# A two-layer hybrid encoder trunk: squares of two token blocks moved up, output-weight splits moved to another loop, and the next layer's norm emitted one token tile later

## The chip, the cores and the metric

One core of one Trainium2 chip runs the whole program in one launch. The metric is the device time of one execution in microseconds. The engines are TensorE (PE; PEld is its weight load), VectorE (DVE), ScalarE (ACT), GpSimd (POOL) and SyncE (SP), which issues most of the transfers.

## What is computed

The input has 1024 tokens of 1024 float32 features. Two layers are applied, each of this form (cut from the reference):

```
h = rms_norm(x, pre_g)
proj = h @ w_in
xa, ga, q_lat, kv_lat, k_rope, gb, u, v, gc = jnp.split(proj, offsets, axis=-1)
ya = rg_lru(causal_depthwise_conv(xa, conv_w, conv_b), ...) * jax.nn.silu(ga)
yb = mla(q_lat, kv_lat, k_rope, positions, ...) * jax.nn.silu(gb)
yc = spatial_gating(u, v, sgu_g, sgu_bn, sgu_w, sgu_b) * jax.nn.silu(gc)
y = jnp.concatenate([rms_norm(ya, g_a), rms_norm(yb, g_b), rms_norm(yc, g_c)], axis=-1)
return x + rms_norm(y @ w_out, post_g)
```

The first branch is a gated linear recurrence of width 384, the second an attention with 6 heads and chunk-causal mask, the third a spatial gate of width 256 that mixes tokens inside blocks of 128. All is float32.

## The kernel before

Every float32 matrix product is made of three matmuls (`mm3`, lines 123 to 126, so the trace shows lines 124, 125, 126): each operand is split into a rounded high part (ScalarE copies it, line 357 or 377) and the rest (a subtraction on GpSimd or VectorE, line 358 or 378), and high x high, high x rest and rest x high are added in PSUM. The banks of PSUM are named pw and pa; tiles in SBUF come from slot pools: F and R with 1024 floats per partition, H with 512, and Y, the array of the branches' outputs, whose rows are lent out as slots while they are free.

A layer goes through these stages; the times are those of layer 0 in the trace, layer 1 follows the same way from about 475 us.

- Prologue, 0 to 43 us. Eight blocks of 128 tokens are loaded (`load_x`), each is normalized (`prenorm`, line 325: squares with a sum on ScalarE at line 317, an inverse root on GpSimd at lines 132 and 133, a scaling on VectorE at line 328), two blocks at a time are transposed (`turn_pair`, line 331: TensorE at 339, evictions on ScalarE at 345 and VectorE at 346). Blocks 4 to 7 (`x4`) come last. The first projection groups then feed a convolution (line 436 on ScalarE, 438 and 441 on VectorE).
- Recurrence and its gates, to 105 us; u and v of the spatial branch, to 149 us. In the loop over the eight token tiles of u and v, `stage_wo` (line 620) loads a block of 128 rows of w_out in an even step and in the odd one splits it and stores both parts in a scratch tensor in device memory. Blocks 5 to 7 also get a gain (line 629).
- The spatial branch's gate, 149 to about 185 us: for each tile eight products, a tanh (716) and a release of the bank by VectorE (717). The same loop stages blocks 4 to 7 of w_out (line 721). Beside it stand the normalization of v (655), its affine step (659, 660), the spatial mixing (`sgu_mix`, 673) and, in layer 0, the rope tables on VectorE (261 to 301).
- Latents, to 215 us; the attention branch's gates, to 256 us: three blocks of gate weights by two halves of the tokens, `feat` and `gate_in` (412, 414), with keys and values made in between.
- Attention, to 400 us. The sums of squares for the attention branch's norm come in at its end (`stats`, line 512: ScalarE 517, sums 520, TensorE 524).
- Output projection, 400 to 475 us: for each of eight tiles `project` (lines 998 to 1013), a gain (1106), the norm over the row (`row_rsqrt`), scaling and residual (1110). In layer 0 the tile is normalized at once for layer 1 and, with its pair, transposed.

The order on each engine is decided by a scheduler of the framework, which reorders instructions by its own estimate of their durations; those marked with `keep` stay in program order. Each engine works through its own instructions in order. The part that stages the weights reads:

```
staged[k] = FS.take((128, 1024)), FS.take((128, 1024))
nc.sync.dma_start(out=staged[k][0], in_=A["w_out"][l, r:r + 128, :])
...
split(st, hi.bitcast(F32R), st.bitcast(F32R), G)
S_.dma_start(out=wo_dram[k][0], in_=hi)
G.dma_start(out=wo_dram[k][1], in_=st)
```

Of the kernel before, what the change touches and what calls it, by code (L numbers as in the profile page):

```python
# [17 lines left out]
NT = T // 128  # L18
# [69 lines left out]
def trunk_kernel(tc, A, out):  # L88
# [236 lines left out]
    def prenorm(xs, ns, order=lambda i: i, last=lambda i: i):  # L325
        r = row_rsqrt(xs, order=order)
        for i, (x, n) in enumerate(zip(xs, ns)):
            last(V.tensor_scalar(out=n, in0=x, scalar1=r[:, i:i + 1], scalar2=None, op0=ALU.mult))
        return ns
# [211 lines left out]
    for i in range(2):  # L541
# [3 lines left out]
                                     3: lambda: prenorm(xn[3:4], xn[3:4], keep)})  # L545
    turn_pair(0, xn[2:], hT, 1, FS)
    turn_params(prow)
    ws[1].split(keep)
    prenorm(x4[:2], x4[:2], keep)
    xn, xs = x4, FS  # L550

    for l in range(DEPTH):
# [35 lines left out]
        if l == 0:  # L588
            prenorm(xn[2:], xn[2:], last=keep)
# [30 lines left out]
        def stage_wo(n):  # L620

            k, r = n // 2, W_ROWS[n // 2]
            if n % 2 == 0:
                staged[k] = FS.take((128, 1024)), FS.take((128, 1024))
                nc.sync.dma_start(out=staged[k][0], in_=A["w_out"][l, r:r + 128, :])
                return
            st, hi = staged.pop(k)
            if k >= 5:
                S_.activation(st, st, AF.Copy, scale=bgain(r // 128))
            split(st, hi.bitcast(F32R), st.bitcast(F32R), G)  # L630
# [80 lines left out]
        for t in range(NT):  # L711
# [9 lines left out]
            stage_wo(8 + t)  # L721
# [327 lines left out]
        for m in range(3):  # L1049
# [6 lines left out]
            for half in range(2):  # L1056
                ps = bank("P1")
                feat(ps, hT, w, 0, half)
                gate_in(ps, YB + m, half)
                if m == 2:  # L1060
# [32 lines left out]
        xn = []  # L1093
        for t in range(NT):
            ts = slice(t * 128, (t + 1) * 128)
            xo = load_x(src, t)
            yh, yl, z = started.pop(t, None) or project(t, 0, 5)
            cols = tile_cols(t)
# [8 lines left out]
            r = row_rsqrt([z], cols)  # L1107
# [5 lines left out]
            if l + 1 < DEPTH:  # L1113
                if t < 4:
                    xn += prenorm([z], [xo])
                    if t % 2:
                        turn_pair(l + 1, xn, hT, t // 2, FS)
                        xn = []
                else:
                    if t == 4:  # L1120
                        for y in yhalf:
                            YS.lend(y)
                        ws = {0: W(l + 1, 0, 256, 4)}
                        xs = YS
                    n = YS.take((128, 2, 512))
                    xn += prenorm([z], [n])
                    FS.give(xo)
            else:
                FS.give(xo)
# [27 lines left out]
```

## Time and profile before

| | |
|---|---|
| median of 3 runs | 928.41 us (928.18 to 929.45) |
| the profiled execution | 924.58 us |
| its span | 922.8 us |
| mean granted TensorE clock | 0.988 of full speed |
| busy PE / PEld | 879.5 / 777.6 us |
| busy DVE / ACT / POOL | 569.9 / 519.8 / 411.6 us |
| moved by DMA | 86.93 MB, 94 GB/s on average |

The profiled execution is one run with records; the span is what the records cover, and 1.8 us of its time lie outside of it. In a row of the timeline the first number is the start, the second the duration, and the brackets at the end give the idle time of the engine ahead of the instruction and what ended it. Matmuls are pipelined, so a row's duration is longer than the distance to the next one. The granted clock is 1.00 at 2.4 GHz and 0.50 at 1.2 GHz.

### The profile page before, as it was taken

What the parts mean: (1) busy time and instruction counts of PE and PEld (TensorE: products, weight loads), DVE (VectorE), ACT (ScalarE), POOL (GpSimd) and SP (SyncE); (2) the same over time, 40 slices, a digit from 0 to 9 for tenths busy, and PEclk for the clock granted to TensorE, in tenths of its full rate; (3) what the DMA queues carried; (4) which work ended last, traced back from release to release, by engine and by line L of the source; (5) the groups of instructions that cost most, each with busy time, mean ns of one, the idle gap of its engine ahead of it and who ended that gap; (6) DMA issues with size and microseconds to landing.
All of it is one profiled execution on the core that took longest, in us unless ns stands there. A gap on an engine that the chain in (4) does not pass through costs nothing. (4 is left out here: it accounts for less than half of the span.)

```text
span 922.8 us, 13671 instructions
## 1 busy us (share of the span) xinstructions
PE 879.5 (95%) x5078; PEld 777.6 (84%) x5078; DVE 569.9 (62%) x1083; ACT 519.8 (56%) x1032; POOL 411.6 (45%) x460
## 2 busy tenths in 40 slices
PE   6799998999999999989999999989989999999996
PEld 5698887998889889867888888889978999988786
DVE  4457965755589897454456488434555989863322
ACT  6445844544767778444544386344466877755312
POOL 3320037464045568384743000666530567656822
PEclk9799999999999999999999999999999999999998
DMA  7200447322000253022324022762200015221322
GB/s 275 56 24 23 137 148 241 134 107 59 14 1 1 93 183 115 23 89 93 116 94 123 1 80 86 292 221 110 59 14 0 1 47 194 80 70 47 127 101 92
DMA packets 45079, 86.93 MB, mean 94 GB/s; under 512 B 8824, under 2 KB 26836, under 8 KB 45012
## 3 DMA queue, kind: packets, MB, share of 16 engines
q1 hardware_dynamic: 35796, 52.50, 17.8%
q0 software_dynamic: 6912, 25.17, 7.8%
q10 hardware_dynamic: 2304, 8.39, 2.3%
q8 instruction: 40, 0.66, 0.3%
q14 instruction: 27, 0.22, 0.1%
HBM read 60.88 MB, written 25.17 MB: 93 GB/s over the span
## 5 line engine op out<-in xcount | busy, mean ns | idle before, releaser
L124 PE MATMUL pw<-R,R 128*128 128x512 f32 (+1 forms) x704 | 258.8, 370 | 10.8 <-DVE Y L441 6.7
L125 PE MATMUL pw<-R,R 128*128 128x512 f32 (+1 forms) x704 | 253.0, 360 | 0.0
L126 PE MATMUL pw<-R,R 128*128 128x512 f32 (+1 forms) x704 | 252.7, 360 | 0.3 <-POOL R L378 0.3
L124 PE MATMUL pa<-R,R 128*128 128x512 f32 (+3 forms) x540 | 187.8, 349 | 9.6 <-DVE Y L717 4.4
L125 PE MATMUL pa<-R,R 128*128 128x512 f32 (+3 forms) x540 | 186.0, 345 | 0.0
L126 PE MATMUL pa<-R,R 128*128 128x512 f32 (+3 forms) x540 | 184.7, 345 | 0.0
L124 PEld LDWEIGHTS pw<-R,R 128*128 128x128 f32 x704 | 134.5, 192 | 31.3 <-issue 6.9
L126 PEld LDWEIGHTS pw<-R,R 128*128 128x128 f32 x704 | 134.5, 191 | 19.1 <-POOL R L378 0.9
L125 PEld LDWEIGHTS pw<-R,R 128*128 128x128 f32 x704 | 135.1, 192 | 17.4
L124 PEld LDWEIGHTS pa<-R,R 128*128 128x128 f32 x540 | 102.1, 189 | 20.6 <-DVE Y L717 4.6
L949 POOL TENSOR_SCALAR F<-F,ring 128x128 f32<-128x128 f32 (+3 forms) x96 | 72.8, 763 | 89.1 <-DVE ring L948 87.7
L126 PEld LDWEIGHTS pa<-R,R 128*128 128x128 f32 x540 | 101.8, 189 | 9.9
L125 PEld LDWEIGHTS pa<-R,R 128*128 128x128 f32 x540 | 102.2, 189 | 8.6
L358 DVE TENSOR_TENSOR R<-pa,R 128x512 fp32r<-128x512 f32 (+1 forms) x120 | 73.9, 630 | 16.7 <-ACT R L357 15.7
L947 ACT ACTIVATE F<-pw,ring 128x128 f32<-128x128 f32 (+3 forms) x96 | 71.1, 743 | 20.8 <-DVE ring L945 18.4
L945 DVE TENSOR_REDUCE ring<-pw 128x1 f32<-128x128 f32 (+3 forms) x96 | 71.6, 749 | 11.3 <-PE pw L938 10.7
L378 POOL TENSOR_TENSOR R<-F,R 128x1024 fp32r<-128x1024 f32 (+1 forms) x23 | 51.1, 2229 | 61.1 <-ACT R L377 36.9
L357 ACT ACTIVATE R<-pa 128x512 fp32r<-128x512 f32 (+1 forms) x120 | 63.8, 554 | 19.2 <-PE pa L969 17.6
L978 PE MATMUL pa<-R,R 128*128 128x256 f32 x480 | 72.1, 288 | 0.5 <-DVE R L358 0.5
L978 PEld LDWEIGHTS pa<-R,R 128*128 128x128 f32 x480 | 63.4, 190 | 3.6 <-DVE R L358 1.1
L969 PE MATMUL pa<-ident,F 128*128 128x128 f32 x432 | 63.6, 273 | 0.4 <-DVE R L358 0.3
L1106 POOL TENSOR_TENSOR F<-F,F 128x1024 f32<-128x1024 f32 (+2 forms) x20 | 39.3, 1966 | 47.6 <-DVE F L1013 47.4
(302 smaller groups left out, 1357.5 us busy)
## 6 DMA issues: line engine op xcount, KB each, us to landing
F<-in_w_in SPq DMA_DIRECT2D x26, 512.0 KB, 4.4
F<-in_x SPq DMA_DIRECT2D x12, 512.0 KB, 4.2
F<-in_w_out SPq DMA_DIRECT2D x9, 512.0 KB, 3.6
F<-x SPq DMA_DIRECT2D x8, 512.0 KB, 4.4
Y<-in_w_out SPq DMA_DIRECT2D x7, 512.0 KB, 4.4
x<-F SPq DMA_DIRECT2D x7, 512.0 KB
out_y<-F SPq DMA_DIRECT2D x7, 512.0 KB
F<-in_w_in SPq DMA_DIRECT2D x7, 352.0 KB, 4.4
```

What stands on the lines that cost most here:

```text
L124: PE.matmul(ps, lhsT=sh, rhs=mh, start=start, stop=False)
L125: PE.matmul(ps, lhsT=sh, rhs=ml, start=False, stop=False)
L126: PE.matmul(ps, lhsT=sl, rhs=mh, start=False, stop=stop)
L357: S_.activation(h, src, AF.Copy)
L358: (eng or G).tensor_tensor(out=lo, in0=src, in1=h.bitcast(F32), op=ALU.subtract)
L378: (eng or self.eng).tensor_tensor(out=lo, in0=st, in1=h.bitcast(F32), op=ALU.subtract)
L945: V.tensor_reduce(out=mx, in_=sv, axis=AX.XY, op=ALU.max, negate=True)
L947: S_.activation(p[:, 0:n].rearrange("p (a b) -> p a b", a=sv.shape[1]), sv, AF.Exp, bias=mx, accum_out=sm)
L949: G.tensor_scalar(out=p[:, 0:n], in0=p[:, 0:n], scalar1=rs, scalar2=1.0, op0=ALU.mult, op1=ALU.mult)
L969: PE.transpose(pv[:, c, i * 128:(i + 1) * 128], p[i][:, b * 128:(b + 1) * 128], ident)
L978: PE.matmul(o, lhsT=sv, rhs=pt[:, part, c * 256:(c + 1) * 256], start=(b == 0 and part == 0), stop=(b == nb - 1 and part == 1))
L1106: G.tensor_tensor(out=zgf[:, c], in0=zf[:, c], in1=gf[:, c], op=ALU.mult)
```

## The change

1. `prenorm` is taken apart into `row_rsqrt` and `scale_rows`. The squares of blocks 4 and 5 now come between the transposes of the two pairs of the prologue, their scaling after the parameters' turning; blocks 6 and 7 keep the squares' place and are scaled after the first projection group. These instructions keep program order.
2. `stage_wo` takes the second slot only when it splits; blocks 4 to 7 are loaded and split in the loop of the attention gates (steps 0 to 3 load, steps 1 to 4 split), no more in the spatial gate's loop. Gain and copy keep program order.
3. In the output projection, what belongs to the next layer's norm moves into `finish(t)`, which is called one tile later, behind that tile's first five products; the row norm keeps program order. The loan of Y's rows and the first weight load of the next layer come a little earlier in tile 4.

```
@@ -322,10 +322,12 @@
                                    op1=ALU.add)
         return rsqrt(ms[:, 0:len(xs)], len(xs))
 
-    def prenorm(xs, ns, order=lambda i: i, last=lambda i: i):
-        r = row_rsqrt(xs, order=order)
+    def scale_rows(xs, ns, r, order=lambda i: i):
         for i, (x, n) in enumerate(zip(xs, ns)):
-            last(V.tensor_scalar(out=n, in0=x, scalar1=r[:, i:i + 1], scalar2=None, op0=ALU.mult))
+            order(V.tensor_scalar(out=n, in0=x, scalar1=r[:, i:i + 1], scalar2=None, op0=ALU.mult))
+
+    def prenorm(xs, ns, order=lambda i: i):
+        scale_rows(xs, ns, row_rsqrt(xs, order=order))
         return ns
 
     def turn_pair(l, xn, hT, pair, slots, then={}, order=lambda i: i):
@@ -543,10 +545,12 @@
     ws[0].split(eng=V, n=1)
     turn_pair(0, xn[:2], hT, 0, FS, {0: lambda: ws[0].split(keep), 1: lambda: prenorm(xn[2:3], xn[2:3], keep),
                                      3: lambda: prenorm(xn[3:4], xn[3:4], keep)})
+    r4 = row_rsqrt(x4[:2], order=keep)
     turn_pair(0, xn[2:], hT, 1, FS)
     turn_params(prow)
+    scale_rows(x4[:2], x4[:2], r4, keep)
     ws[1].split(keep)
-    prenorm(x4[:2], x4[:2], keep)
+    r6 = row_rsqrt(x4[2:], order=keep)
     xn, xs = x4, FS
 
     for l in range(DEPTH):
@@ -586,7 +590,7 @@
 
         group(0, 0)
         if l == 0:
-            prenorm(xn[2:], xn[2:], last=keep)
+            scale_rows(xn[2:], xn[2:], r6, keep)
         hT.append(new_hT())
 
         if l:
@@ -621,13 +625,14 @@
 
             k, r = n // 2, W_ROWS[n // 2]
             if n % 2 == 0:
-                staged[k] = FS.take((128, 1024)), FS.take((128, 1024))
-                nc.sync.dma_start(out=staged[k][0], in_=A["w_out"][l, r:r + 128, :])
+                staged[k] = FS.take((128, 1024))
+                nc.sync.dma_start(out=staged[k], in_=A["w_out"][l, r:r + 128, :])
                 return
-            st, hi = staged.pop(k)
+            st, hi = staged.pop(k), FS.take((128, 1024))
             if k >= 5:
-                S_.activation(st, st, AF.Copy, scale=bgain(r // 128))
-            split(st, hi.bitcast(F32R), st.bitcast(F32R), G)
+                keep(S_.activation(st, st, AF.Copy, scale=bgain(r // 128)))
+            keep(S_.activation(hi.bitcast(F32R), st, AF.Copy))
+            G.tensor_tensor(out=st.bitcast(F32R), in0=st, in1=hi, op=ALU.subtract)
             S_.dma_start(out=wo_dram[k][0], in_=hi)
             G.dma_start(out=wo_dram[k][1], in_=st)
             FS.give(st)
@@ -718,7 +723,6 @@
                                    op0=ALU.add, op1=ALU.mult)
             HS.give(th)
             drain(2)
-            stage_wo(8 + t)
         w.give()
         drain(100)
         HS.give(sg)
@@ -1057,6 +1061,11 @@
                 ps = bank("P1")
                 feat(ps, hT, w, 0, half)
                 gate_in(ps, YB + m, half)
+                step = 2 * m + half
+                if 0 < step < 5:
+                    stage_wo(7 + 2 * step)
+                if step < 4:
+                    stage_wo(8 + 2 * step)
                 if m == 2:
                     for p in hT[half]:
                         for t in p:
@@ -1090,11 +1099,34 @@
         gpost = load_bcast(A["post_norm_g"][l])
         if l + 1 < DEPTH:
             hT = [new_hT()]
-        xn = []
+        xn, zs = [], {}
+
+        def finish(t):
+
+            z, xo = zs.pop(t)
+            if l + 1 < DEPTH:
+                n = xo if t < 4 else YS.take((128, 2, 512))
+                xn.extend(prenorm([z], [n], keep))
+                if t < 4 and t % 2:
+                    turn_pair(l + 1, xn, hT, t // 2, FS)
+                    xn.clear()
+                if t >= 4:
+                    FS.give(xo)
+            else:
+                FS.give(xo)
+            FS.give(z)
+
         for t in range(NT):
             ts = slice(t * 128, (t + 1) * 128)
             xo = load_x(src, t)
             yh, yl, z = started.pop(t, None) or project(t, 0, 5)
+            if t:
+                finish(t - 1)
+            if t == 4 and l + 1 < DEPTH:
+                for y in yhalf:
+                    YS.lend(y)
+                ws = {0: W(l + 1, 0, 256, 4)}
+                xs = YS
             cols = tile_cols(t)
             project(t, 5, 8, (yh, yl, z))
             RS.give(yh)
@@ -1104,30 +1136,14 @@
             for c in cols:
                 c = slice(*c)
                 G.tensor_tensor(out=zgf[:, c], in0=zf[:, c], in1=gf[:, c], op=ALU.mult)
-            r = row_rsqrt([z], cols)
+            r = row_rsqrt([z], cols, keep)
             for c in ((0, 512), (512, 1024)) if t == NT - 1 else cols:
                 c = slice(*c)
                 V.scalar_tensor_tensor(out=zf[:, c], in0=zgf[:, c], scalar=r, in1=xf[:, c], op0=ALU.mult, op1=ALU.add)
                 nc.sync.dma_start(out=(x1_dram if l == 0 else out[0])[ts, c], in_=zf[:, c])
             FS.give(zg)
-            if l + 1 < DEPTH:
-                if t < 4:
-                    xn += prenorm([z], [xo])
-                    if t % 2:
-                        turn_pair(l + 1, xn, hT, t // 2, FS)
-                        xn = []
-                else:
-                    if t == 4:
-                        for y in yhalf:
-                            YS.lend(y)
-                        ws = {0: W(l + 1, 0, 256, 4)}
-                        xs = YS
-                    n = YS.take((128, 2, 512))
-                    xn += prenorm([z], [n])
-                    FS.give(xo)
-            else:
-                FS.give(xo)
-            FS.give(z)
+            zs[t] = z, xo
+        finish(NT - 1)
         for p in wo:
             for t in p:
                 RS.give(t)
```

ScalarE in the prologue (L317 are the squares, H is their scratch output, F and Y hold the blocks; L345 or L347 evicts transposes, L377 or L379 splits weights, L436 or L438 starts the convolution). Before:

```order
L317 ACTIVATE H_143,ring<-F_139 128x1024
L345 ACTIVATE R_101<-pa_66,pg 128x256
L345 ACTIVATE R_103<-pa_67,pg 128x256
...
L377 ACTIVATE R_113<-F_140 128x1024
L377 ACTIVATE R_115<-Y 128x1024
L317 ACTIVATE H_142,ring<-Y 128x1024
L317 ACTIVATE H_143,ring<-Y 128x1024
L317 ACTIVATE H_141,ring<-Y 128x1024
L317 ACTIVATE H_142,ring<-Y 128x1024
L436 ACTIVATE Y<-pw_63,par 128x512
```

And now:

```order
L317 ACTIVATE H_143,ring<-F_139 128x1024
L317 ACTIVATE H_142,ring<-Y 128x1024
L317 ACTIVATE H_143,ring<-Y 128x1024
L347 ACTIVATE R_101<-pa_66,pg 128x256
...
L379 ACTIVATE R_113<-F_140 128x1024
L379 ACTIVATE R_115<-Y 128x1024
L317 ACTIVATE H_142,ring<-Y 128x1024
L317 ACTIVATE H_143,ring<-Y 128x1024
L438 ACTIVATE Y<-pw_63,par 128x512
```

Two squares of blocks held in Y stand ahead of the eight evictions of pair 1, and two, not four, between the weight splits and the convolution.

TensorE in the spatial gate of layer 0 (pw_64 is the gate product of tile 2, pa_65 behind it the spatial mixing). Before:

```order
L126 MATMUL pa_66<-R_115,R_108 128x256
L124 MATMUL pw_64<-R_116,R_101 128x256
L125 MATMUL pw_64<-R_114,R_101 128x256
L126 MATMUL pw_64<-R_116,R_102 128x256
...
L124 MATMUL pa_65<-R_128,R_130 128x256
L125 MATMUL pa_65<-R_129,R_130 128x256
L126 MATMUL pa_65<-R_128,R_130 128x256
L124 MATMUL pw_64<-R_116,R_103 128x256
```

And now:

```order
L126 MATMUL pa_66<-R_115,R_108 128x256
L124 MATMUL pw_64<-R_116,R_101 128x256
L125 MATMUL pw_64<-R_114,R_101 128x256
L126 MATMUL pw_64<-R_116,R_102 128x256
...
L126 MATMUL pw_64<-R_115,R_108 128x256
L124 MATMUL pa_65<-R_128,R_130 128x256
L125 MATMUL pa_65<-R_129,R_130 128x256
L126 MATMUL pa_65<-R_128,R_130 128x256
L124 MATMUL pa_67<-R_125,R_101 128x352
```

The mixing on pa_65, which waits for VectorE's release of that bank (L717, now L722), stands behind 24 matmuls on pw_64 instead of 6.

TensorE at the end of attention in layer 0 (L978 or L982 is attention's last value product, pw the early output projection, L524 or L526 the second sum of squares). Before:

```order
L978 MATMUL pa_68<-R_106,R_118 128x256 x3
L124 MATMUL pw_64<-R_125,R_103 128x512
L125 MATMUL pw_64<-R_126,R_103 128x512
L126 MATMUL pw_63<-R_123,R_108 128x512
...
L126 MATMUL pw_63<-R_101,R_108 128x512
L524 MATMUL pa_66<-ones,H_142 128x1 x4
L126 MATMUL pw_64<-R_125,R_108 128x512
```

And now:

```order
L982 MATMUL pa_68<-R_106,R_118 128x256 x4
L124 MATMUL pw_63<-R_123,R_103 128x512
L125 MATMUL pw_63<-R_109,R_103 128x512
L124 MATMUL pw_64<-R_125,R_103 128x512
L125 MATMUL pw_64<-R_126,R_103 128x512
L526 MATMUL pa_66<-ones,H_143 128x1 x4
L126 MATMUL pw_63<-R_123,R_108 128x512
```

The sum of squares follows the last value product after 4 matmuls; before, 30 stood between the two.

## Rows read from the trace of the kernel before

**Rows 1.** The page, part 1: busy time per engine, share of the span, instructions.

```profile
PE 879.5 (95%) x5078; PEld 777.6 (84%) x5078; DVE 569.9 (62%) x1083; ACT 519.8 (56%) x1032; POOL 411.6 (45%) x460
```

**Rows 2.** TensorE's timeline: start us, us, engine, line, instruction, [idle before <-releaser].

```profile
34.68 0.77 PE L124 MATMUL pw<-R,R 128*128 128x512 f32 x1 [6.69 <-DVE Y L441]
...
160.03 0.58 PE L124 MATMUL pa<-R,R 128*128 128x256 f32 x1 [4.40 <-DVE Y L717]
...
414.93 0.66 PE L339 MATMUL pa<-ident,F 128*128 128x128 f32 x4 [3.92 <-DVE F L328]
...
416.13 0.79 PE L124 MATMUL pw<-R,R 128*128 128x512 f32 x1 [0.54 <-ACT F L1011]
...
499.35 0.39 PE L124 MATMUL pa<-R,R 128*128 128x256 f32 x1 [1.60 <-DVE R L346]
```

**Rows 3.** By stretch: length, busy (count) PE PEld DVE ACT POOL, granted clock, DMA share.

```profile
31.00:40.00 9.00, 5.32 (x13) 4.24 (x14) 5.51 (x11) 0.00 (x0) 0.69 (x1) 0.50 0.01 2
...
160.00:170.00 10.00, 9.97 (x60) 9.97 (x61) 9.31 (x30) 4.69 (x7) 1.36 (x2) 0.83 0.41 131
...
410.00:420.00 10.00, 5.54 (x19) 4.00 (x18) 3.99 (x4) 5.01 (x8) 6.99 (x8) 0.83 0.42 157
...
600.00:620.00 20.00, 17.42 (x133) 16.72 (x132) 7.42 (x16) 8.54 (x13) 14.09 (x11) 1.00 0.64 220
...
670.00:690.00 20.00, 16.61 (x92) 13.98 (x91) 12.19 (x29) 12.58 (x28) 7.07 (x6) 1.00 0.06 15
```

**Rows 4.** ScalarE's timeline, 16 to 31 us.

```profile
19.73 3.03 ACT L345 ACTIVATE R<-pa,pg 128x256 fp32r<-128x256 f32 x8 [2.86 <-PE pa L339]
...
24.50 1.10 ACT L317 ACTIVATE H<-Y 128x1024 bf16<-128x1024 f32 x1
...
28.66 1.49 ACT L436 ACTIVATE Y<-pw,par 128x512 f32<-128x512 f32 x2
```

**Rows 5.** VectorE's timeline, 24 to 41 us.

```profile
31.03 0.15 DVE L438 COPY tails<-pw 128x3 f32<-128x3 f32 x1
```

**Rows 6.** VectorE's timeline, 149 to 163 us: two rope rows and the release.

```profile
157.70 1.69 DVE L275 TENSOR_SCALAR Y<-Y 128x128 f32<-128x128 f32 x1
...
159.56 0.41 DVE L717 SCALAR_TENSOR_TENSOR Y<-H,pa 128x256 f32<-128x256 f32 x1
...
160.94 0.23 DVE L275 TENSOR_SCALAR Y<-Y 128x128 f32<-128x128 f32 x1
```

**Rows 7.** GpSimd's timeline, 149 to 161 us.

```profile
157.64 1.67 POOL L378 TENSOR_TENSOR R<-F,R 128x704 fp32r<-128x704 f32 x1
```

**Rows 8.** VectorE's timeline, 162 to 170 us.

```profile
163.39 1.38 DVE L655 TENSOR_SCALAR F<-F,mv,ring 128x256 f32<-128x256 f32 x4
...
164.89 1.22 DVE L659 TENSOR_TENSOR F<-F,H 128x1024 f32<-128x1024 f32 x1
```

**Rows 9.** By line, duration ns min/median/max: subtraction, copy, gain.

```profile
L358 POOL TENSOR_TENSOR F<-F,F x6: 2378/2406/2410, 131.9 to 631.3; 128x1024 fp32r<-128x1024 f32 x6
...
L357 ACT ACTIVATE F<-F x6: 1058/1061/1064, 129.8 to 626.3; 128x1024 fp32r<-128x1024 f32 x6
...
L629 ACT ACTIVATE F<-F,par x3: 1152/1155/1157, 165.0 to 616.1; 128x1024 f32<-128x1024 f32 x3
```

**Rows 10.** By stretch: the attention gates of layer 0.

```profile
215.00:256.00 41.00, 41.00 (x208) 35.23 (x207) 20.74 (x42) 24.73 (x46) 7.27 (x8) 1.00 0.07 16
```

**Rows 11.** TensorE's timeline: end of attention and the second statistics, layer 0.

```profile
398.96 0.62 PE L978 MATMUL pa<-R,R 128*128 128x256 f32 x3 [0.24 <-DVE R L358]
...
406.27 0.94 PE L524 MATMUL pa<-ones,H 128*128 128x1 f32 x8
```

**Rows 12.** VectorE's sum L520: the timeline at 402 us, and by line.

```profile
402.61 2.11 DVE L520 TENSOR_TENSOR H<-H,H 128x512 f32<-128x512 f32 x1 [0.70 <-ACT H L517]
...
L520 DVE TENSOR_TENSOR H<-H,H x8: 683/1292/2108, 374.0 to 856.8; 128x512 f32<-128x512 f32 x8
```

**Rows 13.** DMA issues from 0 to 20 us: KB each, median us to landing.

```profile
Y<-in_x SPq DMA_DIRECT2D x4, 512.0 KB, 8.8
```

## The prediction

> **What bounds the kernel now.** I began with the busy times: TensorE is busy for 879.5 us of a span of 922.8 [rows 1], so 43.3 us of idling is all that any reordering can save, apart from time at the lower clock. The second view is TensorE's own timeline, for the gaps. The five rows of [rows 2] are long ones, each with its releaser: 6.69 us ahead of the convolution's release in layer 0, 4.40 us in the spatial-gate projection, 3.92 and 0.54 us in the output projection, 1.60 us at the start of layer 1. The rows by stretch add two more places in layer 1: the gate projection of the spatial branch idles 20.00 - 17.42 = 2.58 us, the start of the attention gates 20.00 - 16.61 = 3.39 us [rows 3]. The third thing to see is in the same rows: after the three longest gaps the granted clock stood at 0.50 (31 to 40 us) or averaged 0.83 over ten microseconds, that is the 1.2 GHz level for a part of them, while the stretches with gaps of 1.6 us or less show 1.00. At 0.83 a gap costs another 0.17 x 10 = 1.7 us, because TensorE advances at half speed.
>
> The profiled execution took 924.58 us, 3.83 below the median of 928.41. All terms below are differences; I subtract them from the median.
>
> **Squares of blocks 4 and 5 (layer 0, prologue).** ScalarE idles 2.86 us before the transposes' evictions of pair 1 at 19.73. The four squares begin at 24.50 and the convolution's first instruction follows them at 28.66, so a square takes 4.16 / 4 = 1.04 us [rows 4]. Two fit into the gap (2.1 of 2.86 us). Then only two stand ahead of the convolution, which can start when the last matmul ends, at 34.68 - 6.69 = 27.99. VectorE's first convolution copy comes one such instruction (1.49 / 2 us) later, near 28.8, instead of at 31.03 [rows 5], since the scalings in front of it are done early too. Every later step moves with it: **-2.2 us**. The clock stays low until about 40 whatever restarts at 34.68; a shorter gap could bring it back sooner or never lower it, worth up to half of the 5.3 us from 34.68 to 40. Bounds: 0 (the data come too late for the gap) and -4.9.
>
> **Output weights 4 to 7 (layer 0).** Their load, gain, copy, subtraction and stores leave the spatial-gate loop. Of the 4.40 us gap there, VectorE's release came at 159.56, behind rope operations. One of these took 1.69 us at 157.70, the same line at 160.94 took 0.23 [rows 6]; the long one ran exactly beside GpSimd's weight split of 157.64 to 159.31 [rows 7]. The Trainium skill, GPSIMD Engine Reference, section Specifications, says GpSimd's path to SBUF is shared with VectorE and contended when VectorE runs in a two-port mode or reads two SBUF inputs. The row agrees: 1.69 against 0.23 us; by that rule the moved subtractions take such holds with them to the new stage, by the bare instruction times they don't (a rival below). In the new order TensorE has 24 matmuls on bank pw ahead of the spatial mixing instead of 6: 18 more at 17.42 / 133 = 0.13 us [rows 3] are 2.4 us of cover. But VectorE now has four normalizations (1.38 us) and an affine product (1.22 us) [rows 8] ahead of its first releases. I take 2.0 us of gaps left and the clock kept up: 4.4 + 1.7 - 2.0 = **-4.1**, between -6.1 (no gap) and 0 (a gap as long as before). Layer 1 loses the same work, from the stretch with 2.58 us idle: **-1.5**, between -2.6 and 0.
>
> **The same work in the attention gates' loop.** ScalarE gets per layer four copies of 1.06 and three gains of 1.15 us: 7.7 us. GpSimd gets four subtractions of 2.41 us, 9.6 us [rows 9], and the issues of four stores. In layer 0 TensorE has no idle time there, ScalarE is busy 24.73 and GpSimd 7.27 of 41 us [rows 10]. There is room (32.4 of 41), and three banks between TensorE and its readers cover a single delay. I take +0.5 for layer 0. Layer 1's counterpart has 3.39 us of gaps, which another order of VectorE and ScalarE may shorten or repeat; I take -1.0. Together **-0.5**, between -4 and +4.
>
> **The norm one tile later.** The gaps of 3.92 and 0.54 us and the clock behind them (1.7) go: 6.2 us. The next wait comes from the order. Before, the second statistics product (L524) stood 30 matmuls of the early projection behind attention's last value product (L978); it ran at 406.27 and waited for nothing. Now four stand between, and the last L978 ended at 398.96 + 0.62 = 399.58 [rows 11]. The 30 took (406.27 - 399.58) / 30 = 0.22 us each, so four end near 400.5; its operand comes from VectorE's sum L520, which ends at 402.61 + 2.11 = 404.7 [rows 12]. That is a new gap of 4.2 to 4.4 us, longer than the one that lowered the clock: 4.4 + 1.7 = 6.1 lost against 6.2 saved. When the held projection is over (43 matmuls, some 10 us, and the clock), near 417, the scaled tile that ended the old gap at 414.93 is there and the transposes wait for nothing. So **0**. This sum of VectorE takes between 0.68 and 2.11 us [rows 12]; if short, and the clock holds, the term is -6.2 + 3.0 = -3.2. If one more reader is late it is +1.5.
>
> **Start of layer 1.** Transposes of the last pair are split and 24 weight matmuls put ahead, which covers the 1.60 us and smaller waits; the scaling of tile 7 now stands behind the gates' weight split on VectorE, a wait of about 1.7 us in exchange. I take **-0.6**, between -2.4 and +1. Attention is only reshuffled: 0, within 1.5 either way, judged by the single waits of a few tenths there. The end of layer 1 keeps its order. The loads of the output weights move on SyncE's queue into a stage with 7% DMA share [rows 10]; the third block of gate weights now stands behind two of them, but two blocks' matmuls come before it is needed: 0. On GpSimd's queue the last subtraction stands behind a memset that waits for TensorE and ahead of the first scaling of attention: at most 2.4 us and an issue, within the bounds of the gates' term.
>
> Sum: -2.2 - 4.1 - 1.5 - 0.5 + 0 - 0.6 = -8.9, so 928.4 - 8.9 = **919.5 us**.
>
> **Rivals.**
> - *Deeper.* The clock never falls at the new statistics gap (-1.7), comes back early in the prologue (-2.7) and the spatial gate has no gap (-2.0): 919.5 - 6.4 = 913.1. For it: gaps up to 1.6 us left the clock at 1.00. Against: 3.92 us lowered it. Chance 0.07.
> - *VectorE's queue in the spatial gate.* The normalizations and both affine steps (1.38 + 1.22 + about 1.2 = 3.8 us) all end before the first release; the gap stays 3.8 and lowers the clock: the term is 4.4 - 3.8 = -0.6 instead of -4.1: 923.0. For it is the order, against it the 2.4 us of cover. Chance 0.13.
> - *The squares don't fit.* The loads of x need 8.8 us to landing under full DMA [rows 13]; if blocks 4 and 5 come after 18, ScalarE, which runs in order, holds up the evictions of pair 1. With the term at +1 instead of -2.2 it gives 922.7. Chance 0.05.
> - *Slower.* GpSimd's eight subtractions hold VectorE in the gates' loop as the split held L275, and in-order VectorE holds the releases of TensorE's banks and the first scores. Fully exposed they cost 8 x 2.41 = 19.3 us. From 8.9 / 19.3 = 46% exposed the change loses; with two thirds exposed the time is 919.5 + 12.9 = 932.4. For it: the wide rope row. Against: VectorE idles half of this stage, and only instructions like weight scalings are open to it, not the gates' own. Chance 0.13.
> - *No change.* The new waits, each sized above, come out at their upper bounds (0 for the spatial gate, +4 for the gates' loop, -2.2 and -1.5 kept): within 0.2%, which is about what a measurement of this kernel can tell from none. Chance 0.07.
>
> **Numbers.** The forecast has the remaining 0.55. Faster by over 0.2%: 0.55 + 0.07 + 0.13 + 0.05 = 0.80; the same 0.07; slower 0.13. For the range, the bounds of the prologue (2.7 down, 2.2 up) and of the spatial gate (2.0 down, 4.1 up) weigh most. Below it reaches to 912.5, the deeper case with 0.6 more; above to 929.0, past the no-change case, leaving out the slower one and a little at the bottom.
>
> **What would show it.** Right: TensorE's gap at the convolution is near 4.5 us, restarting near 32.5; no gap over 2 us in the spatial gate and no 0.50 there; a gap of 4 us in front of the second L526 (was L524) with the low clock behind it, and none at the transposes. Wrong: gaps over 1 us in the attention gates of layer 0, or POOL subtractions with VectorE instructions of 2 us beside them; a gap at the pair-1 evictions; the first scores later than before relative to the last gate matmul.

## The result, and the profile after

The changed kernel takes 943.03 us in the median of four runs (940.34 to 944.29); the kernel before takes 928.29 in four (925.91 to 929.45). The ratio is 1.0145, 95% interval 1.0121 to 1.0169: **slower by 14.7 us, where 919.5 was forecast and 929.0 was the upper end of the range**.

The profiled execution of the changed kernel took 944.29 us (span 942.5), that of before 924.58. So the two traces differ by 19.7 us, 5 more than the medians, and single steps below are good to an us or two, those of layer 1 to less (see behind the table). The page of the changed kernel, part 1, answers to [rows 1]:

```profile
span 942.5 us, 13695 instructions
PE 889.7 (94%) x5078; PEld 784.1 (83%) x5078; DVE 585.8 (62%) x1083; ACT 522.8 (55%) x1032; POOL 409.0 (43%) x460
```

TensorE has the same 5078 matmuls and is 10.2 us longer busy: more of them ran at the lower clock (a mean granted clock of 0.982; it was 0.988). Its idle time grew from 43.3 to 942.5 - 889.7 = 52.8 us. VectorE has the same 1083 instructions as before and is 585.8 - 569.9 = 15.9 us longer busy: instructions of the same kinds and sizes take longer. That is the odd number of this page, and the experiments turn on it.

In the lines of the changed kernel, L359 and L360 (for weights L379 and L380) are the copy and the subtraction of a split, L634 and L635 those of a staged block of w_out. L810 and L811 split the transposed latents, L888 and L889 the keys; L994 is the product that ends a unit of attention.

The longer waits of TensorE's timeline (start, duration, engine, line, instruction, idle before and its releaser), after; the first, second and sixth stand where the first three of [rows 2] stood:

```profile
32.76 0.77 PE L124 MATMUL pw<-R,R 128*128 128x512 f32 x1 [5.11 <-DVE Y L443]
157.37 0.39 PE L124 MATMUL pa<-R,R 128*128 128x256 f32 x1 [2.44 <-DVE Y L722]
228.86 0.66 PE L802 MATMUL pa<-ident,F 128*128 128x128 f32 x4 [1.17 <-DVE R L811]
260.00 0.69 PE L124 MATMUL pa<-R,R 128*128 128x384 f32 x1 [4.08 <-DVE R L889]
363.52 0.30 PE L973 MATMUL pa<-ident,F 128*128 128x128 f32 x1 [2.75 <-DVE R L360]
412.65 0.33 PE L526 MATMUL pa<-ones,H 128*128 128x1 f32 x1 [3.97 <-DVE H L522]
686.78 0.50 PE L124 MATMUL pa<-R,R 128*128 128x512 f32 x1 [1.16 <-DVE Y L416]
```

By stretch (from:to, length, busy and count of PE, PEld, DVE, ACT, POOL, granted clock, DMA share, GB/s), behind these waits:

```profile
255.00:266.00 11.00, 6.92 (x25) 6.21 (x23) 8.19 (x14) 6.04 (x16) 3.49 (x4) 0.69 0.24 95
360.00:370.00 10.00, 7.22 (x43) 6.87 (x43) 8.46 (x17) 5.44 (x13) 6.59 (x12) 0.83 0.44 150
410.00:420.00 10.00, 7.35 (x22) 6.17 (x23) 4.20 (x4) 2.72 (x5) 8.93 (x10) 0.66 0.04 14
680.00:700.00 20.00, 18.29 (x82) 14.46 (x82) 12.04 (x23) 12.72 (x21) 6.64 (x6) 0.91 0.49 151
815.00:830.00 15.00, 12.15 (x76) 10.96 (x75) 11.32 (x23) 9.63 (x23) 10.59 (x17) 0.89 0.46 141
```

The waits at 260.00 and 363.52, and the low clock at 815 to 830, have no counterpart before. The averages below 1.00 show that TensorE worked a part of each stretch at 1.2 GHz.

**Where the time went.** Both kernels issue the same matmuls. I give each matmul its shape's spacing at full clock and add up ("by equal work"); the sum is the same in both, some 855 to 860 us by how the spacing is read, and the time at which each kernel reaches the same part of it shows where it fell behind:

| step | forecast | by the traces |
|---|---|---|
| prologue | -2.2 | -2.6 |
| spatial gate and latents, layer 0 | -4.1 | -0.9 |
| attention gates and start of attention, layer 0 | +0.5 | +10.1 |
| attention, layer 0 | 0 | +2.5 |
| norm one tile later | 0 | +0.4 |
| start of layer 1 | -0.6 | -0.5 |
| layer 1 through its spatial gate | -1.5 | -1.9 |
| attention gates, layer 1 | -1.0 | +4.2 |
| attention, layer 1 | 0 | +6.4 |
| end of layer 1 | 0 | +2.0 |
| sum | -8.9 | +19.7 |

The profiled execution of before was quick in layer 1. Experiment 11 has the same order of instructions there, and by equal work falls 3.4 us behind it between 605 and 693. The rows of layer 1 are good to no more than that.

### The profile page after: what moved, and what is told of

Its sections match the earlier page's. It is cut to its first block, busy times and chain, and to the rows that moved or that the text cites. A ratio compares the mean times of both kernels' runs of the same rounds, so it can differ in the third digit from the quotient of the medians.

```text
span 942.5 us, 13695 instructions
## 1 busy us (share of the span) xinstructions
PE 889.7 (94%) x5078; PEld 784.1 (83%) x5078; DVE 585.8 (62%) x1083; ACT 522.8 (55%) x1032; POOL 409.0 (43%) x460
## 4 chain that ended last, share of the span: by engine, by line
PE 50%; DVE 11%; ACT 6%; issue 3%; DMA 2%; POOL 1%; DVEq 0%; POOLq 0%; ACTq 0%; SPq 0%
PE pw L124 9%; PE pw L126 9%; PE pw L125 9%; PE pa L982 5%; PE pa L973 4%; PE pa L124 4%; PE pa L125 4%; PE pa L126 4%; DVE R L360 2%; DMA F<-in_w_in 2%; DVE ring L949 1%; ACT F L951 1%; DVE Y L994 1%; PE pw L942 1%; ACT R L359 1%
## 5 line engine op out<-in xcount | busy, mean ns | idle before, releaser
L124 PEld LDWEIGHTS pa<-R,R 128*128 128x128 f32 x540 | 102.8, 191 | 25.4 <-DVE R L889 5.6
L126 PEld LDWEIGHTS pa<-R,R 128*128 128x128 f32 x540 | 102.7, 191 | 10.1
L125 PEld LDWEIGHTS pa<-R,R 128*128 128x128 f32 x540 | 103.0, 191 | 8.9
L380 POOL TENSOR_TENSOR R<-F,R 128x1024 fp32r<-128x1024 f32 (+1 forms) x23 | 51.8, 2255 | 84.2 <-ACT R L379 61.0
L360 DVE TENSOR_TENSOR R<-pa,R 128x512 fp32r<-128x512 f32 (+1 forms) x120 | 73.6, 629 | 22.1 <-ACT R L359 20.9
L982 PE MATMUL pa<-R,R 128*128 128x256 f32 x480 | 75.8, 294 | 0.1
L359 ACT ACTIVATE R<-pa 128x512 fp32r<-128x512 f32 (+1 forms) x120 | 62.9, 553 | 18.6 <-PE pa L973 16.0
L973 PE MATMUL pa<-ident,F 128*128 128x128 f32 x432 | 65.5, 276 | 4.9 <-DVE R L360 4.8
L982 PEld LDWEIGHTS pa<-R,R 128*128 128x128 f32 x480 | 66.5, 196 | 3.1 <-DVE R L360 0.7
L1138 POOL TENSOR_TENSOR F<-F,F 128x1024 f32<-128x1024 f32 (+2 forms) x20 | 39.2, 1962 | 54.1 <-DVE F L1017 52.9
```

What stands on the lines that cost most here:

```text
L124: PE.matmul(ps, lhsT=sh, rhs=mh, start=start, stop=False)
L125: PE.matmul(ps, lhsT=sh, rhs=ml, start=False, stop=False)
L126: PE.matmul(ps, lhsT=sl, rhs=mh, start=False, stop=stop)
L359: S_.activation(h, src, AF.Copy)
L360: (eng or G).tensor_tensor(out=lo, in0=src, in1=h.bitcast(F32), op=ALU.subtract)
L380: (eng or self.eng).tensor_tensor(out=lo, in0=st, in1=h.bitcast(F32), op=ALU.subtract)
```

## The experiments

**What VectorE did at the two new waits.** VectorE's timeline before the wait of 260.00, after:

```profile
255.20 0.68 DVE L889 TENSOR_TENSOR R<-pa,R 64x512 fp32r<-64x512 f32 x1 [1.59 <-ACT R L888]
256.80 2.42 DVE L360 TENSOR_TENSOR R<-H,R 128x512 fp32r<-128x512 f32 x1 [0.92 <-ACT R L359]
259.25 0.69 DVE L889 TENSOR_TENSOR R<-pa,R 64x512 fp32r<-64x512 f32 x1
...
261.36 0.69 DVE L360 TENSOR_TENSOR R<-H,R 128x512 fp32r<-128x512 f32 x1
```

and GpSimd's, the same stretch:

```profile
256.33 2.34 POOL L635 TENSOR_TENSOR F<-F,F 128x1024 fp32r<-128x1024 f32 x1 [3.03 <-ACT F L634]
258.62 0.30 POOL L977 MEMSET R<- 128x256 f32 x1
```

L360, a split of 512 columns, takes 0.69 us at 261.36 and 2.42 at 256.80, where the moved subtraction of GpSimd (L635) runs from 256.33 to 258.67. The held L360 ends at 259.22, that is 0.55 after it. L889 stands behind it on VectorE, and TensorE waits for L889. The hold makes 1.7 of the 4.08 us. On ScalarE the moved copy stands right ahead of L359, the copy that this L360 waited for:

```profile
255.19 1.06 ACT L634 ACTIVATE F<-F 128x1024 fp32r<-128x1024 f32 x1
256.15 0.61 ACT L359 ACTIVATE R<-H 128x512 fp32r<-128x512 f32 x1
```

The wait of 363.52, VectorE then GpSimd, after:

```profile
358.14 0.42 DVE L991 SCALAR_TENSOR_TENSOR H<-pa,H 64x256 f32<-64x256 f32 x1
358.59 3.72 DVE L994 TENSOR_TENSOR Y<-Y,H 64x256 f32<-64x256 f32 x1
362.23 0.54 DVE L949 TENSOR_REDUCE ring<-pw 128x1 f32<-128x384 f32 x1
362.70 1.13 DVE L360 TENSOR_TENSOR R<-pa,R 128x512 fp32r<-128x512 f32 x2
```

```profile
358.69 2.10 POOL L953 TENSOR_SCALAR F<-F,ring 128x896 f32<-128x896 f32 x2
360.77 1.25 POOL L360 TENSOR_TENSOR R<-H,R 128x512 fp32r<-128x512 f32 x1
361.98 0.60 POOL L1024 DMA_DIRECT2D R<-wo5h  x1
```

And the same product in the kernel before, VectorE:

```profile
353.42 0.42 DVE L990 TENSOR_TENSOR Y<-Y,H 64x256 f32<-64x256 f32 x1
```

The product of attention's unit 16 (counted from 0) took 0.42 us and takes 3.72 beside three GpSimd instructions on end, until their end at 362.02 and 0.29 more. A reduction and the L360 that TensorE waits for stand behind it. In layer 1 the same product took 3.02 us, beside the same three:

```profile
817.10 3.02 DVE L994 TENSOR_TENSOR Y<-Y,H 64x256 f32<-64x256 f32 x1
```

It was not touched by the change: the scheduler, which had a new set of instructions to place upstream, set it beside that train.

The theory **A** of what follows: part 2 of the change (the output weights 4 to 7) is the whole loss, by VectorE instructions held for the length of the GpSimd instructions beside them. Rival **B**: by the copies and gains on ScalarE, which stand ahead of its own evictions (at 225.84 a moved copy of 1.05 us runs just ahead of L810, on which L811 and the wait of 228.86 rest; the copy at 255.19 above is another). Rival **C**: by the new order in attention as such, whatever lies beside what.

**1. Without the move.** Parts 1 and 3 alone; the staging of blocks 4 to 7 as before:

```
-                step = 2 * m + half
-                if 0 < step < 5:
-                    stage_wo(7 + 2 * step)
-                if step < 4:
-                    stage_wo(8 + 2 * step)
...
             drain(2)
+            stage_wo(8 + t)
```

> The changed kernel with part 2 undone: output weights 4 to 7 are staged in the spatial gate's loop again, parts 1 (squares) and 3 (norm later) stay. All theories that blame part 2 expect the attention start and attention as before: prologue -2.6 us, output stage +0.4, start of layer 1 -0.5, so 925 to 926 us against 928.3 before. If parts 1 or 3 cost the time, it stays above 935.

Measured: 927.52 us (12 runs) beside 929.65 for before, ratio 0.9974 (0.9958 to 0.999). By equal work it is 2.0 us ahead of before all the way from the gates to the output projection. There the wait for the transposes is still 3.89 us long (at 412.93), where 3.92 stood before [rows 2]: part 3 by itself did nothing to it.

**2. The move alone.** The kernel before with part 2.

> The kernel before with part 2 alone. If part 2 makes the whole loss, 943.0 + 2.7 = 945 to 946 us; if it needs part 1 or 3 beside it, 928 to 935.

Measured: 945.33, ratio 1.0162 (1.0127 to 1.0197). Part 2 is the whole loss, and more: 1.0162 x 0.9974 = 1.0136, within the interval of the full change. TensorE waits 3.97 us for the second sum of squares here as in the full change: it is part 2 that put this wait in the place of the transposes', by way of the scheduler. The time fits A, B and C alike. Part 2 also makes the copies of all eight blocks keep program order and takes the second slot later; no run separates that from the move.

**3. The staged subtractions on VectorE.** This frees the gates' stage of GpSimd's long instructions. The line serves all eight blocks of a layer, so the four that were not moved go to VectorE too, sixteen in all.

```
-            G.tensor_tensor(out=st.bitcast(F32R), in0=st, in1=hi, op=ALU.subtract)
+            V.tensor_tensor(out=st.bitcast(F32R), in0=st, in1=hi, op=ALU.subtract)
```

> The changed kernel with the staged subtraction on VectorE (some 1.2 us each) instead of GpSimd; the order in attention is unchanged. Theory A (GpSimd's subtraction of 2.4 us holds VectorE): the VectorE rows of 2.4 us in the attention gates' loop shrink to 0.7, the gap at attention's start in layer 0 falls from 4.1 to 2.2 us or less and the clock stays up there, 3 to 5 us gained in layer 0 and 1 to 3 in layer 1: 935 to 939 us. Theory B (ScalarE's copies and gains ahead of the key evictions): the gap stays near 4 us, 942 to 945. Theory C (the new order in attention): its loss of 2.7 and 6.9 us inside attention stays in both cases.

Measured: 942.05, ratio 1.0132 (1.0104 to 1.0161): a miss in time; the interval overlaps that of the change. The hold is gone, as VectorE's timeline shows at the same place:

```profile
256.48 1.22 DVE L635 TENSOR_TENSOR F<-F,F 128x1024 fp32r<-128x1024 f32 x1 [0.46 <-ACT F L634]
257.63 0.68 DVE L360 TENSOR_TENSOR R<-H,R 128x512 fp32r<-128x512 f32 x1
258.34 0.69 DVE L889 TENSOR_TENSOR R<-pa,R 64x512 fp32r<-64x512 f32 x1
```

L360 is back at 0.68 us and the wait of 4.08 is gone. But one grew upstream, on TensorE, and lowered the clock there:

```profile
229.67 0.55 PE L802 MATMUL pa<-ident,F 128*128 128x128 f32 x3 [1.96 <-DVE R L811]
227.00:240.00 13.00, 10.46 (x34) 7.87 (x34) 7.20 (x8) 6.28 (x10) 3.02 (x2) 0.74 0.77 226
```

The product of unit 16 is still held, for 3.68 us. By equal work the place gains 6.4 us against the change, and the chain upstream (L810, L811) loses 3.3 more. So the subtraction's hold was real, but a good half of what it cost in that one place was paid at another.

**4. The copies and gains on GpSimd.** This takes all the moved work off ScalarE, and the copies of the four blocks that were not moved with it.

```
-                keep(S_.activation(st, st, AF.Copy, scale=bgain(r // 128)))
-            keep(S_.activation(hi.bitcast(F32R), st, AF.Copy))
+                G.tensor_scalar(out=st, in0=st, scalar1=bgain(r // 128), scalar2=None, op0=ALU.mult)
+            G.tensor_copy(hi.bitcast(F32R), st)
```

> The changed kernel with gain and copy of the moved weights on GpSimd instead of ScalarE; the order of attention in layer 0 is unchanged. Theory B: with ScalarE freed of 7.7 us the gap at attention's start in layer 0 falls from 4.1 to below 2 us. Theory A: GpSimd works longer, VectorE is held at more places, the gap is as long or longer, and the time is 943 us or more.

Measured: 945.22 (two runs), ratio 1.0167 (1.0127 to 1.0207): no gain. But the sign that had been set for B did come: at attention's start in layer 0, where the change has the wait of 4.08 us, TensorE has none over 0.2, and by equal work the 7 us lost there are gone. The time stayed up because other waits grew; the longest stands in the spatial gate of layer 0, where GpSimd now also has the copy of a block that was not moved:

```profile
167.10 0.58 PE L124 MATMUL pa<-R,R 128*128 128x256 f32 x1 [5.04 <-DVE Y L722]
```

L360 is held less at attention's start too (1.62 us at 252.87), since GpSimd's subtractions come at other times. So this run doesn't tell A from B at that place, and it can't be read as "B has no part": it shows that GpSimd is no better home for the copies.

**5. Unit 16's product on GpSimd.** One number leaves the table of products that VectorE takes.

```
-Y_ON_V = (2, 4, 5, 6, 8, 9, 13, 14, 16, 19, 20, 21, 23)
+Y_ON_V = (2, 4, 5, 6, 8, 9, 13, 14, 19, 20, 21, 23)
```

> The changed kernel with attention's product of unit 16 on GpSimd instead of VectorE (0.74 us there); the order of the rest in attention is unchanged. In the changed kernel this product took VectorE 3.72 us in layer 0 and 3.02 in layer 1, beside back-to-back GpSimd work, against 0.42 before. Theory A (GpSimd holds VectorE): the gaps behind it (2.75 us at 361, 1.07 and 1.36 at 816 to 821) and the two clock falls of 3.4 us vanish, 7 to 9 us: 934 to 937 us. Theory C (the new order as such): the gaps stay, 941 to 944.

Measured: 933.47 (10 runs), ratio 1.0043 (1.0026 to 1.0061). Against the change that is 943.03 - 933.47 = 9.6 us, from one product of 0.42 us that is run once per layer. In attention of layer 0 every engine's order is otherwise the same up to 369, so C is out there. By stretch, the places of both holds:

```profile
355.00:370.00 15.00, 14.66 (x106) 13.47 (x105) 12.83 (x29) 13.02 (x31) 14.45 (x21) 1.00 0.45 142
810.00:830.00 20.00, 18.71 (x132) 17.09 (x131) 15.63 (x34) 15.91 (x36) 16.29 (x23) 1.00 0.40 132
```

The clock stays at 1.00 in both. By equal work 4.2 us come back at the first place and 3.4 at the second. Behind the second, from 827, the scheduler changed the order as well, and the 2.0 us that the table has at the end of layer 1 are gone there. The wait at the start of attention is still there (4.47 us at 261.31). This is the strongest run for A.

**6. Both, 3 and 5.**

> Both: the staged subtraction on VectorE and the product of unit 16 on GpSimd, part 2 otherwise as in the changed kernel. If the two holds add up: 942.0 - 7 to 9 = 933 to 936 us, and what is left against the kernel before lies in the attention gates' loop, about 4 to 6 us. If the first gives way to another wait: 938 or more.

Measured: 931.52 (10 runs), ratio 1.0022 (1.0007 to 1.0037), 2.0 us less than experiment 5, which was measured beside it. So of the 15.9 us that part 2 costs (1.0145 against 0.9974) the two edits take away 11.4, most of it by the product. What is left against experiment 1, 1.0022 - 0.9974 = 0.5% or 4.5 us (give or take 2), comes from neither hold. An estimate from the traces says that it comes from no more holding at all. I add up what VectorE's instructions took above the median of their kind, shape and tiles: 27 us before, 30 in experiment 1, 42 after the change, 43 in experiment 2, 34 in 3 and in 5, and 28 here.

Where the rest stands, by equal work: layer 0 loses 4.2 us in the gates' loop, where L802 waits 1.96 us at 228.24 for L811, and ahead of L811 ScalarE has the moved copy (1.05 us) and VectorE the moved subtraction (1.23 us). Layer 1 loses 2.2 in its gates' loop and 3.9 in attention up to 815, in small waits. B names a part of this; so may the eight subtractions that this edit needlessly put on VectorE. It was not taken apart further.

Experiments 7 to 10 start from experiment 1 and ask whether the two waits that part 2 and part 3 were aimed at can be had in another way.

**7. Subtractions of blocks 4 to 7 on VectorE, in their old place.**

```
-            split(st, hi.bitcast(F32R), st.bitcast(F32R), G)
+            split(st, hi.bitcast(F32R), st.bitcast(F32R), V if k >= 4 else G)
```

> Part 2 undone (as in the run without the move), and the subtractions of blocks 4 to 7, in the spatial gate's loop, on VectorE instead of GpSimd; attention's order is unchanged. Theory A: the release of the bank there no longer waits behind held rope rows, the gap of 4.4 us falls below 2.5 and the clock stays up: 3 to 5 us, 922.5 to 924.5 us against 927.5. If the gap comes from ScalarE or the tanh, it stays: 927 to 929, or 1 to 2 more for VectorE's longer work.

Measured: 930.22 (12 runs), ratio 1.0007 (0.9987 to 1.0027): a miss; the wait became longer. One of VectorE, then GpSimd, then TensorE:

```profile
156.07 1.76 DVE L261 CAST ring<-pos_i 128x8 f32<-128x8 int32 x1
156.11 1.68 POOL L380 TENSOR_TENSOR R<-F,R 128x704 fp32r<-128x704 f32 x1
158.61 0.58 PE L124 MATMUL pa<-R,R 128*128 128x256 f32 x1 [5.18 <-DVE Y L721]
```

A cast of eight columns is now the one held, by another GpSimd instruction, the split of the projection's weights; it takes 0.16 us elsewhere. And VectorE pays for the subtraction itself, 1.62 us at 153.60. This execution (934.42) lay above the median, and by equal work loses more in layer 1, 6.3 us about a wait of 3.21 at 626.81; that was not followed up.

**8. Rope tables two tiles later**, so that no rope row stands ahead of the release.

```
-        if l == 0:
-            rope_tables()
...
+            if l == 0 and t == 2:
+                rope_tables()
```

> Part 2 undone, and the rope tables of layer 0 emitted inside the spatial gate's loop after its third tile, so that VectorE's first two releases come ahead of all rope rows. If the gap of 4.4 us there comes from rope rows that GpSimd's weight split holds (1.7 of 1.9 us of waiting), it falls to 2.6 us or less and the clock stays up: 2 to 4 us, 923.5 to 925.5 against 927.5. If it comes from ScalarE's tanh or from the weights' landing, it stays above 4 us: 927 to 928.

Measured: 931.74 (8 runs), ratio 1.0027 (1.0016 to 1.0037): a miss. The wait is 4.67 us, now for ScalarE's tanh behind its own staged copies, and the rope rows are held in their new place. VectorE, then GpSimd:

```profile
167.68 2.44 DVE L280 SCALAR_TENSOR_TENSOR Y<-Y 128x128 f32<-128x128 f32 x1
170.05 2.38 DVE L284 TENSOR_SCALAR Y<-Y 128x128 f32<-128x128 f32 x1
```

```profile
167.57 2.40 POOL L360 TENSOR_TENSOR R<-F,R 128x1024 fp32r<-128x1024 f32 x1 [4.52 <-ACT R L359]
169.94 2.40 POOL L380 TENSOR_TENSOR R<-F,R 128x1024 fp32r<-128x1024 f32 x1
```

L280 takes 0.29 us at 175.99; here it and L284 take 2.4 each, every time beside one GpSimd subtraction of 2.40 us. By equal work the spatial gate of layer 0 loses 7.4 us.

**9. As 8, and two splits of the output projection on VectorE**, in both layers.

```
-            split(Y[:, a:b, ts], yh[:, a:b], yl[:, a:b], G)
+            split(Y[:, a:b, ts], yh[:, a:b], yl[:, a:b], V if t in (2, 3) and a == 5 else G)
```

> The same, and in the output projection the second split of tiles 2 and 3 on VectorE, so that GpSimd reaches the row norm of tile 0 two splits (some 2.2 us) earlier; the gap of 3.9 us ahead of the transposes there came from that norm. Expected: the gap falls to about 1.7 us, the clock stays up, 3 to 4 us more: 920 to 922 us. If VectorE's sum or ScalarE's squares are the limit instead, nothing is gained over the run with the rope tables later.

Measured: 936.29 (6 runs), ratio 1.0074 (1.0059 to 1.0088). In layer 0 the wait for the transposes falls from 3.9 to 0.57 us, with the clock at 1.00 behind it. The output stage of layer 0 gains 3.3 us by equal work. In layer 1 the same edit makes a wait of 7.01, and costs nearly 8 us there:

```profile
871.23 0.80 PE L124 MATMUL pw<-R,R 128*128 128x512 f32 x1 [7.01 <-ACT F L1015]
```

GpSimd ran five other splits on end there, 5.34 us from 862.35, ahead of a row norm's inverse root; why the order came out so was not followed up.

**10. Experiment 1 with that split on VectorE in layer 0 alone**, rope tables in their old place.

```
-            split(Y[:, a:b, ts], yh[:, a:b], yl[:, a:b], G)
+            split(Y[:, a:b, ts], yh[:, a:b], yl[:, a:b], V if l == 0 and t in (2, 3) and a == 5 else G)
```

> Parts 1 and 3 without part 2, and in layer 0 alone the second split of tiles 2 and 3 of the output projection on VectorE. The run before this one had the gap ahead of the transposes down from 3.9 to 0.6 us with the clock up, 4.6 us in all, and lost 7 us at the same edit in layer 1, which is left out here. Expected: 927.5 - 4.6 = 923 us (922 to 924.5), the fastest kernel so far. If the gain there was luck of one execution: 926 to 928.

Measured: 920.91 (4 runs, 919.95 to 922.07) beside 930.05 for before, ratio 0.99 (0.9886 to 0.9913): **faster than both kernels**. TensorE's wait for the transposes, and the stretch around it:

```profile
411.08 0.65 PE L341 MATMUL pa<-ident,F 128*128 128x128 f32 x4 [0.58 <-DVE F L327]
405.00:425.00 20.00, 18.70 (x92) 14.66 (x90) 9.83 (x12) 9.71 (x18) 9.96 (x15) 1.00 0.32 113
```

Before, the ten microseconds from 410 averaged 0.83 [rows 3]. By equal work the output stage of layer 0 is 4.8 us ahead behind this wait and 3.2 at its end, and the prologue gains its 2. That is not all of the 9 us. Against experiment 1 (0.9974) the ratio is 6.9 us better, and of the 5.9 us between the two traces 4.0 lie in layer 1, where every engine has the same order in both. Why layer 1 ran faster here the runs don't show.

**11. The squares alone** (part 1 on the kernel before).

> The kernel before with part 1 alone. By the trace of the changed kernel the prologue gains 2.0 to 2.6 us, nothing else moves: 926.5 to 927.5 us where before has 929.5. If part 3 makes the gain of the run without part 2, this is within 0.2% of before, 928.5 to 930.

Measured: 927.63 (12 runs), ratio 0.9982 (0.9967 to 0.9997), 1.7 us; the wait at the convolution is 5.01 us at 32.45 instead of 6.69.

## Why the prediction was wrong

**The squares** (-2.2) were right: -2.6 in the trace, 1.7 (0.3 to 3.1) by experiment 11.

**The norm one tile later** (0) was right, to the detail: the new wait stands ahead of the second L526, with 3.97 us where 4.2 to 4.4 were foretold, and the low clock behind it. That the change only trades one wait for another of the same length holds. The sum that ends the new wait is itself held, beside a GpSimd gain (L1138) that runs from 409.52 to 412.05; it takes 0.68 us alone [rows 12]:

```profile
410.54 2.05 DVE L522 TENSOR_TENSOR H<-H,H 128x512 f32<-128x512 f32 x1 [0.70 <-ACT H L519]
```

What I had wrong is where the trade comes from: the new order is part 2's doing (experiments 1 and 2), not that of the part which names the norm.

**The spatial gate** (-4.1) failed on the step that one gap of 2.0 us is all that is left behind the cover of 24 matmuls. The gap came as forecast, and two more behind it. VectorE's queue, the named rival, is the reason for the first two, made longer by a hold. VectorE, then GpSimd, after:

```profile
152.05 3.46 DVE L660 TENSOR_SCALAR F<-F,mv,ring 128x256 f32<-128x256 f32 x4 [0.48 <-POOL ring L133]
...
156.91 0.40 DVE L722 SCALAR_TENSOR_TENSOR Y<-H,pa 128x256 f32<-128x256 f32 x1
157.24 2.38 DVE L665 TENSOR_TENSOR F<-F,H 128x1024 f32<-128x1024 f32 x1
```

```profile
151.99 2.40 POOL L635 TENSOR_TENSOR F<-F,Y 128x1024 fp32r<-128x1024 f32 x1
155.69 2.85 POOL L380 TENSOR_TENSOR R<-F,R 128x704 fp32r<-128x704 f32 x1 [1.29 <-ACT R L379]
```

The four normalizations took 1.38 us before [rows 8] and 3.46 here, beside the subtraction of an earlier block. The wait of 2.44 us was near the 2.0 that I took, and the clock stayed at 1.00 in 160 to 170; but waits of 1.17 us (for VectorE's next release) and 1.16 (for ScalarE, in the rope tables) followed up to 168, and the step gained 0.9 where 4.1 were forecast. The rival had said 0.6, but with one gap of 3.8 and the low clock behind it.

**The gates' loop** (-0.5, at most +4) is the first large error: 10.1 + 4.2 = 14.3 us by the traces. I held against the "slower" rival that "only instructions like weight scalings are open to it, not the gates' own". The stage doesn't end with the gates: the first splits of attention (L360 on two SBUF operands) already stand in VectorE's queue there, and one of them was held with L889 behind it; in layer 1 two such L360 took 2.63 and 2.47 us, at 700.62 and 713.73. These were the signs of being wrong that the prediction names. The rival's mechanism was right and its price wasn't: even with all eight subtractions exposed in full it comes to 928.4 - 8.9 + 19.3 = 938.8, and yet experiment 3 shows that taking them off GpSimd gives back only 1.2 us (ratios 1.0145 and 1.0132, whose intervals overlap). The larger part stood in another stage. What stays with both holds gone, some 4.5 us by experiment 6, stands in layer 0 at the chain of the transposed latents (L810, L811), and "there is room (32.4 of 41)" could not show it: the room is an average over the stage and that chain is a place in it.

**Attention "only reshuffled: 0, within 1.5 either way"** is the second, and the larger by experiment: experiment 5 gives back 9.6 us, the end of layer 1 with it. I judged it by the waits that attention had before, as though a reshuffle kept their sizes. I did not ask which VectorE instruction would come to lie beside which GpSimd instruction; the order after, which I had, shows the neighbours on each engine and not across engines.

**The end of layer 1** (0) cost 2.0 us by the traces. Experiments 2 and 3 have the loss too; experiments 5 and 6, which free the held product, don't, but neither does experiment 4, where it is held for 3.86 us in layer 1. What makes the loss stays open.

The rule that I did cite, the Trainium skill's GPSIMD Engine Reference, section Specifications, has the contention with VectorE instructions in a two-port mode or with two SBUF inputs. What I missed is its length. The Trainium skill, SBUF — State Buffer, section Who interferes with whom, says that the port pair is locked for the whole instruction of whoever came first and that the other one blocks fully, and it names casts and `tensor_scalar` among those that can contend. The rows agree: a cast of eight columns took 1.76 us, a `tensor_scalar` 2.38, each beside one GpSimd subtraction of that length; L722, with one operand in PSUM, took its 0.40 beside L380. They go further in one point: L994 was held through three GpSimd instructions, 3.72 us, not until the first one's end, although its record starts 0.10 us ahead of the first; in layer 1 it began inside the first and ended 0.29 us behind the third. And in one point they fall short of the page: beside GpSimd's L133, a `tensor_tensor` of two to eight columns, VectorE's `tensor_tensor` L789 was not held:

```profile
205.29 1.67 POOL L133 TENSOR_TENSOR ra<-ring,mhalf 128x8 f32<-128x8 f32 x1
206.11 0.23 DVE L789 TENSOR_TENSOR F<-rt 128x64 f32<-128x64 f32 x1
```

## What to carry to other kernels

Before you move GpSimd work, list which VectorE instructions read only SBUF in the stage it goes to and in the next, and price each one in front of a release of TensorE as the whole GpSimd instruction, or the whole train of them. Where a scheduler sets the order, price a move by the places at which its new order differs anywhere in the program: 0.42 us of untouched work per layer, in the next stage, cost 9.6 us. At a wait that is to go, try first the smallest edit on the engine that ends it, and in each layer apart: two splits put on VectorE in layer 0 gained some 3 us in their stage, and the same edit in layer 1 lost nearly 8.

## What was not expected of the hardware

- A short VectorE instruction is held to the end of the GpSimd instruction beside it, whatever its own size: 0.16 to 0.69 us became 1.76 to 3.72. In the trace of the changed kernel 22 VectorE `tensor_tensor` with both inputs in SBUF began inside a GpSimd instruction with more time left than they take alone. 16 ended behind it; the other six all lay beside L133 and took their 0.22 to 0.25 us.
- It also goes the other way, though this was only read from rows: GpSimd's L380 at 155.69 took 2.85 us for 704 columns, and 1.71 at 148.86; a VectorE product of 1.21 us on SBUF operands had begun at 155.64.
- Short waits can lower the clock, and not always: behind waits of 1.33 and 1.55 us at 678.11 and 680.64 the kernel before kept a granted clock of 1.00 from 680 to 685; behind the same two (1.33 and 1.54 us, at 678.04 and 680.56) experiment 11, which changes nothing behind the prologue, shows 0.66. So waits of up to 1.6 us left the clock at 1.00 in some executions only, and executions with the same order in layer 1 differ by some us there: 3.4 here, 4.4 between experiments 1 and 10 (605 to 693).
